# A hybrid encoder: the combination of three attention groups asked for later and spread between an item's stages, the gates' tanh and product taken apart, and a recurrence's output products six matmuls later

## The chip, the cores and the metric

The kernel runs on one core of one Trainium2 chip. The time is that of one execution on the device in microseconds, and smaller is better. The core has a matrix engine (TensorE, PE), a vector engine (VectorE, DVE), an activation engine (ScalarE, ACT), a general one (GpSimd, POOL), and SyncE (SP), which here only issues transfers. Each engine takes its own instructions strictly in order; semaphores hold an instruction back until what it needs is there.

## The reference, cut to what matters

Two request groups (1024 and 512 tokens of width 1024) go through two layers. Layer 0 is attention in three dilated groups, whose outputs are combined by a softmax over their log-sum-exps, times a SiLU gate. Layer 1 is a bidirectional complex-diagonal state-space recurrence in 64 groups.

```
def dilated_mixer(h, w_in, w_out):
    proj = h @ w_in
    z = proj[..., 3 * N_DIL * ATTN_WIDTH:]
    for g, (window, dil) in enumerate(DILATED_PAIRS):
        ...
        q = apply_rope(qkv[:, :, 0], cos, sin) * scale
        k = apply_rope(qkv[:, :, 1], cos, sin)
        o, lse = dilated_window_attention(q, k, v, dil, window // (2 * dil))
        outs.append(o)
        lses.append(lse)
    weights = jax.nn.softmax(jnp.stack(lses, axis=0), axis=0)
    o = jnp.einsum('gbsh,gbshe->bshe', weights.astype(h.dtype), jnp.stack(outs, axis=0))
    y = o.reshape(bsz, s, ATTN_WIDTH) * jax.nn.silu(z)
    return y @ w_out

def s5_mixer(...):
    ...
    _, states = lax.associative_scan(_linear_recurrence, (a, bu), axis=1, reverse=(direction == 1))
    y = y + jnp.real(jnp.einsum('bsgp,gcp->bsgc', states, c_mat))
    g = jax.nn.gelu(y)
    y = g * jax.nn.sigmoid(g @ w_glu)
    return (y * jax.nn.silu(z)) @ w_out
```

## The kernel before

**Order of work.** The program writes its order out by hand. A `Timeline` holds items; one item is a block of 24 matmuls of a projection on TensorE (`gemm`, the tile `mm`), with 25 places ("slots") between them. `H(item, slot, function)` hangs a piece of other work at a slot, and the pieces are emitted there, in this order, on whichever engines they use. So a slot number sets the place of an instruction in the queue of its engine, not its time. A slot beyond 24 is counted on into the following items: slot 199 of an item is slot 24 of the seventh item after it.

**Layer 0.** The 16 heads are worked in eight pairs p. For each pair come group 0, group 1, group 2 (12 items each, T = 0 to 11) and then three items of the gate z ("group 3", units (p, 3)). Each attention item hangs its own chain into the items behind it: rope at slot 24 (VectorE's products `t`, GpSimd's sums, L899 and L900, and later the values `ve` and `vs`), the transposed queries and keys at 38 (TensorE's `qkT`, ScalarE's copies, VectorE's low parts `qT` and `kT`, L969 and L971, and GpSimd's casts `kT`), scores `sc` at 76, softmax at 79, transposed weights `eT` and `et` from 100, the product with the values `pv` at 118, and six matmuls later ScalarE's `pw` and `u` and GpSimd's add of `u` (L1082). In the steady stretch, one item after the other, several such chains interleave. The weights of a next unit come as raw tiles (`wraw`, SyncE, L829) and are split into a high part (ScalarE, `whl`, L841) and a low part (VectorE or GpSimd, L844). `u01` and `U` hold the three groups' outputs of a pair; the next pair's group 1 writes its columns of them item by item.

**Combination of a pair.** Once the last item of group 2 has its softmax sums, `combine_load` fetches the statistics of all three groups (`cst`). `combine_prep` has three parts: the minimum and the exponential (ScalarE, `cd`), the division, and a transposition (TensorE, tile `ada`) whose copy `ft` is stored to DRAM; then `f_load` asks for the coefficients `f` of the first chunk, spread over the partitions, in two halves. The tile `f` (128 x 3 x 512) exists once. `combine` treats the tokens in three chunks c = 0, 1, 2 of 512, each in four parts: part 0 multiplies `f` by group 1's output (VectorE, L1165), part 1 by group 0's (VectorE, L1168) and adds (GpSimd, L1169), part 2 by group 2's (VectorE, L1178) and adds (GpSimd, L1179), part 3 multiplies by the gate into `y` (VectorE, L1185), stores `y`, and asks for the next chunk's `f`. This runs beside the next pair's group 1, for p = 0 to 6; the last pair's combination is part of the output projection (`out_proj0`) and hangs elsewhere.

**Gates.** `stage_silu` of a gate item computes tanh on ScalarE into `zs` and right behind it a product on VectorE.

**Layer 1.** For each of the 64 recurrence groups, twelve matmuls apart, `layer1` hangs five steps: inputs `s_b` (0), `s_pre` (1), the scan `s_scan` (9), `s_post` (18) and the output products `s_y` (30), which read the states `sS`. A GLU and an output projection follow.

**Output projection of layer 0.** `out_proj0` hangs the splitting of eight weight blocks (`w_cvt`, L1460 on VectorE) between the last pair's combination parts.

Of the kernel before, what the change touches and what calls it, by code (L numbers as in the profile page):

```python
# [10 lines left out]
F32 = mybir.dt.float32  # L11
# [3 lines left out]
AF = mybir.ActivationFunctionType  # L15
ALU = mybir.AluOpType
# [4 lines left out]
KT = 8  # L21
# [119 lines left out]
class Kern:  # L141
# [550 lines left out]
    def attention(self):  # L692
        nc, I, tl = self.nc, self.I, self.tl
        H = tl.hook
# [8 lines left out]
        for u, (p, g) in enumerate(units):  # L703
            first = at_unit[p, g] = len(tl.items)
            n = NT if g < 3 else 3
            for T in range(n):
                if u == 0 and T < 2:
                    tl.idle(1)
                    i = T
                else:  # L710
                    i = tl.add(self.gemm, (p, g, T))
                if g < 3:
# [6 lines left out]
                    for nm, (ds_, sl) in at.items():  # L719

                        ds_, sl = at[nm] = divmod(max(25 * ds_ + sl, end_of), 25)
# [4 lines left out]
                    if T == NT - 1:  # L726
                        st = divmod(25 * at["soft"][0] + at["soft"][1] + LATER["soft"][0], 25)
                        H(i + st[0], st[1], self.stats_out, p, g)
                        if g == 0:
                            H(i + at["pv"][0] + (at["pv"][1] + LATER["pv"][1] + 1) // 25, (at["pv"][1] + LATER["pv"][1] + 1) % 25, self.u0_store, p)  # L730
                        if end:
                            H(i + st[0], st[1], self.combine_load, p)
                            for k, sl in enumerate((4, 10, 16)):
                                H(i + 3, sl, self.combine_prep, p, k)
                        elif g == 2:
                            H(i + st[0], st[1], self.combine_load, p)
                            for k, sl in enumerate((110, 120, 135)):
                                H(i + sl // 25, sl % 25, self.combine_prep, p, k)
                            for c in range(3):
                                for k, (ds_, sl) in enumerate(((0, 10), (0, 22), (1, 14), (1, 24))):  # L740
                                    H(i + 6 + 3 * c + ds_, sl, self.combine, p, c, k)
                            H(i + 16, 2, self.u0_load, p + 1)
                elif u + 1 < len(units) or T < n - 1:
                    H(i, 24, self.stage_silu, p, T)
            last = i
            if u + 1 == len(units):
                continue
# [350 lines left out]
        dst = D_[1024:1536].rearrange("(i r) c -> i r c", r=4)[:, :, 4 * g:4 * g + 4]  # L1098
        nc.sync.dma_start(dst, st[:, 8:12].rearrange("p r a b -> p r (a b)"))

    def stage_silu(self, p, c):

        nc, A, B = self.nc, self.pools.get("A"), self.pools.get("B")
        ps = self.state.pop(("ps", (p, 3, c)))
        th = self.sb(self.pools["B"], [128, 512], F32, "zs", bufs=3)
        nc.scalar.activation(th, ps, AF.Tanh, scale=0.5)
        nc.vector.scalar_tensor_tensor(th, th, 1.0, ps, op0=ALU.add, op1=ALU.mult)
        self.zs[(p, c)] = th

    def combine_load(self, p):  # L1110
        sc = self.sb(self.pools["B"], [128, NT, 3, 2, 2], F32, "cst", bufs=1)
# [294 lines left out]
    def out_proj0(self):  # L1406


        nc, I, tl = self.nc, self.I, self.tl
        H = tl.hook  # L1410
# [88 lines left out]
        ps = {}  # L1499
# [62 lines left out]
        H(z, 24, y_cvt, 8, nc.vector, 4, P)  # L1562
        H(z, 24, y_cvt, 9, None, 4, P)
        H(z, 24, gates)
        for k, sl in zip(range(2, KT), (0, 8, 21, 35, 47, 52)):
            H(base + sl // 25, sl % 25, w_cvt, k)
        H(base + 47 // 25, 47 % 25, y_cvt, 10)
        H(base + 54 // 25, 54 % 25, y_cvt, 11)
# [59 lines left out]
    def layer1(self):  # L1628

        nc, I, tl = self.nc, self.I, self.tl  # L1630
        H = tl.hook
# [314 lines left out]
            at(T0 + 4 * R * hb - (26 if hb < 2 else 46), u_load, hb)  # L1946
            at(T0 + 4 * R * hb + 3 * R + 44, g_store, hb)
        for g in range(64):
            for off, fn in ((-24, par_load), (0, s_b), (1, s_pre), (9, s_scan), (18, s_post), (30, s_y)):
                at(T0 + R * g + off, fn, g)  # L1950

        def s_end():
# [10 lines left out]
        for n, T in enumerate(order):  # L1963
            s = base6 + 2 * n
            for h in range(2):
                if T == last and h == 1:
                    i = tl.add(lambda m: [mm_last(1 + m // 12, 2 * (m % 12) + e) for e in range(2)])
                else:
                    i = tl.add(mm1, T, h)
# [49 lines left out]
```

## Time and profile before

| | |
|---|---|
| median of 3 runs | 3045.18 us (3042.79 to 3051.17) |
| the profiled execution's own time | 3043.34 us |
| its span, first to last instruction | 3041.2 us |
| TensorE busy | 2771.2 us (91% of the span) |
| VectorE busy | 2149.5 us (71%) |
| ScalarE busy | 1700.9 us (56%) |
| GpSimd busy | 1618.1 us (53%) |
| mean granted TensorE clock | 0.976 of full speed |

Busy shares are averages over stages. What a change in one stage is worth is read from the waits in that stage. In the rows further down, a number in square brackets is the time for which the engine had stood idle before the instruction, with what ended the idle time; an instruction without a bracket followed its predecessor.

### The profile page before, as it was taken

Reading aid. Unit: us, or ns where it says so; the run is one execution under the profiler, and the core shown is the slowest. Engines: PE = TensorE matmul, PEld = TensorE weight load, DVE = VectorE, ACT = ScalarE, POOL = GpSimd, SP = SyncE. Lnnn points to the kernel's source line nnn. Section 1 sums busy time; section 2 is a strip of 40 time slices with the busy share of each in tenths; the row PEclk is TensorE's granted clock in tenths of the full one; section 3 lists DMA queues with packets and bytes.
Section 4 is the critical chain, followed back from the end, with each engine's and each line's share of the span. In section 5 each row is a group of like instructions: output and inputs, shape, how many; then the busy total and the mean of one; then the engine's idle time right before and its main releaser. Section 6 shows DMA issues by size and latency. Waiting matters only on the chain. (4 is left out here: it accounts for less than half of the span.)

```text
span 3041.2 us, 52468 instructions
## 1 busy us (share of the span) xinstructions
PE 2771.2 (91%) x16181; PEld 2414.7 (79%) x16181; DVE 2149.5 (71%) x6071; ACT 1700.9 (56%) x5120; POOL 1618.1 (53%) x2657
## 2 busy tenths in 40 slices
PE   6899999997898989989898998989899998889998
PEld 5798888886787878888787888888688666567887
DVE  7777887775875767677676767767643889975345
ACT  5876777777665757656565666756453222223221
POOL 3765655555764545556464645546463665542243
PEclk8999999998999999999999999999999999999999
DMA  7122333321222222222212122122644554536454
GB/s 210 58 85 85 93 91 89 91 81 29 60 69 70 60 59 63 59 56 57 69 44 73 50 69 65 51 59 55 170 132 134 182 164 149 163 130 190 161 158 132
DMA packets 428232, 293.78 MB, mean 97 GB/s; under 512 B 140288, under 2 KB 379152, under 8 KB 427824
## 3 DMA queue, kind: packets, MB, share of 16 engines
q1 hardware_dynamic: 427808, 290.16, 33.5%
q8 instruction: 129, 2.11, 0.3%
q14 instruction: 151, 1.24, 0.1%
q10 hardware_dynamic: 144, 0.26, 0.0%
HBM read 204.72 MB, written 85.62 MB: 95 GB/s over the span
## 5 line engine op out<-in xcount | busy, mean ns | idle before, releaser
L886 PE MATMUL mm<-whl,hp 128*128 128x384 f32 x4584 | 999.7, 355 | 4.7 <-ACT hp L356 2.8
L886 PEld LDWEIGHTS mm<-whl,hp 128*128 128x128 f32 x4584 | 809.3, 198 | 24.5 <-issue 11.5
L886 PE MATMUL mm<-whl,hs 128*128 128x384 f32 x2304 | 492.0, 347 | 0.0
L886 PEld LDWEIGHTS mm<-whl,hs 128*128 128x128 f32 x2304 | 393.4, 190 | 7.5 <-issue 7.2
L975 POOL CAST kT<-kT 64x128 fp32r<-64x128 f32 x576 | 171.4, 298 | 359.3 <-ACT kT L966 340.1
L969 DVE SCALAR_TENSOR_TENSOR qT<-qkT,qT 64x128 fp32r<-64x128 f32 x576 | 166.2, 289 | 271.3 <-ACT kT L966 265.2
L1082 POOL TENSOR_TENSOR u<-u,pw 128x128 f32<-128x128 f32 x384 | 184.7, 481 | 217.2 <-ACT u L1078 201.6
L1649 PE MATMUL mm<-hp,wi 128*128 128x512 f32 x1104 | 279.5, 401 | 1.8 <-ACT sig L1686 1.8
L1010 ACT ACTIVATE e<-e,st 128x128 f32<-128x128 f32 (+2 forms) x576 | 249.4, 435 | 48.3 <-DVE st L1025 43.6
L1649 PEld LDWEIGHTS mm<-hp,wi 128*128 128x128 f32 x1104 | 202.6, 188 | 53.3 <-issue 8.6
L1077 ACT ACTIVATE pw<-pv 64x256 f32<-64x256 f32 x576 | 218.0, 378 | 46.9 <-PE pv L1068 30.5
L964 ACT ACTIVATE qT<-qkT 64x128 fp32r<-64x128 f32 x576 | 156.3, 271 | 150.7 <-PE qkT L952 144.4
L951 PE MATMUL qkT<-ident,t 128*128 128x128 f32 x288 | 89.1, 309 | 124.4 <-POOL t L900 122.8
L899 POOL TENSOR_TENSOR t<-t,t 128x128 f32<-128x128 f32 x288 | 138.6, 481 | 87.7 <-DVE t L916 71.3
L951 PEld LDWEIGHTS qkT<-ident,t 128*128 128x128 f32 x288 | 40.6, 141 | 174.9 <-POOL t L900 173.4
L942 ACT ACTIVATE vs<-mm 64x128 fp32r<-64x128 f32 (+1 forms) x350 | 95.9, 274 | 148.5 <-DVE t L916 145.7
L1055 DVE TENSOR_TENSOR et<-eT,et 128x512 fp32r<-128x512 f32 (+1 forms) x288 | 163.6, 568 | 14.9 <-ACT et L1053 14.9
L971 DVE TENSOR_TENSOR kT<-qkT,kT 64x128 fp32r<-64x128 f32 x576 | 166.2, 289 | 9.8
L1348 DVE TENSOR_TENSOR f<-f,p_pb 128x4 f32<-128x4 f32 (+6 forms) x448 | 163.6, 384 | 4.0 <-POOL f L1337 0.9
L1053 ACT ACTIVATE et<-eT 128x512 fp32r<-128x512 f32 (+1 forms) x288 | 144.7, 503 | 38.4 <-PE eT L1043 27.6
L841 ACT ACTIVATE whl<-wraw 128x384 fp32r<-128x384 f32 (+1 forms) x224 | 112.6, 507 | 95.8 <-DMA wraw<-in_attn_w_in 91.5
L966 ACT ACTIVATE kT<-qkT 64x128 fp32r<-64x128 f32 x576 | 156.8, 272 | 10.6
(367 smaller groups left out, 6259.7 us busy)
## 6 DMA issues: line engine op xcount, KB each, us to landing
wraw<-in_attn_w_in SPq DMA_DIRECT2D x192, 192.0 KB
par<-par_d SPq DMA_DIRECT2D x64, 512.0 KB
f<-f_d SPq DMA_DIRECT2D x44, 384.0 KB
par_d<-zs SPq DMA_DIRECT2D x64, 256.0 KB
U<-in_ada_w SPq DMA_DIRECT2D x16, 768.0 KB
par_d<-f SPq DMA_DIRECT2D x64, 128.0 KB
raw<-in_ssm_w_in SPq DMA_DIRECT2D x14, 512.0 KB
u_d<-u SPq DMA_DIRECT2D x8, 768.0 KB
```

Of the source, the lines that this page charges most:

```text
L886: nc.tensor.matmul(ps[:, :384], self.hv(a, k, self.tok_cols(g, T)), self.wt[((p, g), k)][:, b], start=m == 0, stop=m == 23)
L964: nc.scalar.activation(qT[r, h], tp[r, 0:128], AF.Copy, scale=-0.125)
L966: nc.scalar.activation(kT[r, 0, h, c], tp[r, 128:256], AF.Copy)
L969: nc.vector.scalar_tensor_tensor(qT[o, h], tp[r, 0:128], -0.125, qT[r, h].bitcast(F32), op0=ALU.mult, op1=ALU.subtract)
L971: nc.vector.tensor_tensor(kT[r, 1, h, c], tp[r, 128:256], kT[r, 0, h, c].bitcast(F32), op=ALU.subtract)
L975: nc.gpsimd.tensor_copy(kT[o, 0, h, c], kT[r, 0, h, c].bitcast(F32))
L1010: nc.scalar.activation(e[:, h, :W], e[:, h, :W], AF.Exp, scale=-1.0, bias=st[:, T, h, 0:1], accum_out=st[:, T, h, 1:2])
L1055: nc.vector.tensor_tensor(et[:, 1, 0:n], tp[:, 0:n], et[:, 0, 0:n].bitcast(F32), op=ALU.subtract)
L1077: nc.scalar.activation(w[hi], pv[hi, h], AF.Copy)
L1082: nc.gpsimd.tensor_tensor(u, u, w[:, a], op=ALU.add)
L1348: v.tensor_tensor(o, x, y, op=op)
L1649: nc.tensor.matmul(st["ps"], state[("w", u)][a][:, k], self.hv(b, k, slice(512 * c, 512 * c + 512)), start=m == 0, stop=m == 23)
```

## The change

Slot numbers change for `combine_prep`, `combine`, one `w_cvt` and `s_y`, and `stage_silu` is called in two halves. No computation is added or removed.

```
 elif g == 2:
     H(i + st[0], st[1], self.combine_load, p)
-    for k, sl in enumerate((110, 120, 135)):
+    for k, sl in enumerate((120, 134, 145)):
         H(i + sl // 25, sl % 25, self.combine_prep, p, k)
     for c in range(3):
-        for k, (ds_, sl) in enumerate(((0, 10), (0, 22), (1, 14), (1, 24))):
-            H(i + 6 + 3 * c + ds_, sl, self.combine, p, c, k)
+        for k, sl in enumerate(((184, 195, 209, 220), (245, 270, 295, 309), (345, 370, 384, 395))[c]):
+            H(i + sl // 25, sl % 25, self.combine, p, c, k)
...
-    H(i, 24, self.stage_silu, p, T)
+    H(i, 24, self.stage_silu, p, T, 0)
+    H(i + 1, 8, self.stage_silu, p, T, 1)
```

```
 # out_proj0, weight blocks 2 to 7
-for k, sl in zip(range(2, KT), (0, 8, 21, 35, 47, 52)):
+for k, sl in zip(range(2, KT), (0, 8, 9, 35, 47, 52)):
     H(base + sl // 25, sl % 25, w_cvt, k)
 # layer1
-for off, fn in ((-24, par_load), (0, s_b), (1, s_pre), (9, s_scan), (18, s_post), (30, s_y)):
+for off, fn in ((-24, par_load), (0, s_b), (1, s_pre), (9, s_scan), (18, s_post), (36, s_y)):
     at(T0 + R * g + off, fn, g)
```

Written as slots from the last item of group 2, `combine` stood at 160, 172, 189, 199 for chunk 0, at 235, 247, 264, 274 for chunk 1, and at 310, 322, 339, 349 for chunk 2. In `stage_silu`, half 0 is the tanh and half 1 the product; the last pair's last gate item still calls both at once. After the change the lines from 1083 on stand one to two further down, so L1165 of before is L1167 of the change, L1168 is L1170, L1169 is L1171, L1179 is L1181, L1185 is L1187, L1082 is L1083 and L844 is L845.

The first place is VectorE's queue where the coefficients of the first pair leave: `ft` is their copy, `qT` and `kT` are the low parts of an item's queries and keys, and `t` are rope's products of the next. Before:

```order
1940 L1141 COPY ft<-ada 72x128
1941 L969 SCALAR_TENSOR_TENSOR qT<-qkT,qT 64x128 x2
1942 L971 TENSOR_TENSOR kT<-qkT,kT 64x128 x2
1943 L915 TENSOR_TENSOR t_12817<-mm,rope 128x256
1944 L916 TENSOR_TENSOR t_12818<-mm,rope 128x256
```

and now:

```order
1940 L970 SCALAR_TENSOR_TENSOR qT<-qkT,qT 64x128 x2
1941 L972 TENSOR_TENSOR kT<-qkT,kT 64x128 x2
1942 L1143 COPY ft<-ada 72x128
1943 L916 TENSOR_TENSOR t_12817<-mm,rope 128x256
1944 L917 TENSOR_TENSOR t_12818<-mm,rope 128x256
```

The copy, and with it the store and the load of `f` behind it, moved behind the low parts.

The second place is VectorE's queue from chunk 0's part 3 (`y`) to chunk 1's part 0 (L1165, later L1167) of the same pair; `e,st` rows of the softmax stand in the gaps. Before:

```order
1963 L1185 SCALAR_TENSOR_TENSOR y<-f,zs 128x512
1964 L915 TENSOR_TENSOR t_12943<-mm,rope 128x256
...
1973 L969 SCALAR_TENSOR_TENSOR qT<-qkT,qT 64x128 x2
1974 L971 TENSOR_TENSOR kT<-qkT,kT 64x128 x2
1975 L915 TENSOR_TENSOR t_13024<-mm,rope 128x256
...
1983 L895 TENSOR_TENSOR vs<-mm,vs 64x128
1984 L1165 TENSOR_TENSOR f<-f,u_693 128x512
1985 L969 SCALAR_TENSOR_TENSOR qT<-qkT,qT 64x128 x2
```

and now:

```order
1974 L1187 SCALAR_TENSOR_TENSOR y<-f,zs 128x512
1975 L916 TENSOR_TENSOR t_13024<-mm,rope 128x256
...
1983 L896 TENSOR_TENSOR vs<-mm,vs 64x128
1984 L970 SCALAR_TENSOR_TENSOR qT<-qkT,qT 64x128 x2
1985 L972 TENSOR_TENSOR kT<-qkT,kT 64x128 x2
1986 L1167 TENSOR_TENSOR f<-f,u_693 128x512
1987 L916 TENSOR_TENSOR t_13108<-mm,rope 128x256
```

Part 3 stands one item later than before against the same rope pieces (`t_13024`), part 0 a few rows later; so one item's pieces lie between the two where there were one and a half.

The third place is GpSimd's queue at the end of chunk 2 of the first pair, where a weight tile is split (`whl`). Before, both of chunk 2's adds (L1169, L1179) stood further up:

```order
783 L899 TENSOR_TENSOR t_13447<-t_13447,t_13448 128x4x32
784 L900 TENSOR_TENSOR t_13447<-t_13447,t_13448 128x4x32
785 L975 CAST kT<-kT 64x128 x2
786 L1082 TENSOR_TENSOR u_693<-u_693,pw 128x128 x2
787 L899 TENSOR_TENSOR t_13525<-t_13525,t_13526 128x4x32
788 L900 TENSOR_TENSOR t_13525<-t_13525,t_13526 128x4x32
789 L844 TENSOR_TENSOR whl<-wraw,whl 128x384
790 L975 CAST kT<-kT 64x128 x2
```

and now:

```order
783 L976 CAST kT<-kT 64x128 x2
784 L1171 TENSOR_TENSOR f<-f 128x512
785 L1083 TENSOR_TENSOR u_693<-u_693,pw 128x128 x2
786 L900 TENSOR_TENSOR t_13520<-t_13520,t_13521 128x4x32
787 L901 TENSOR_TENSOR t_13520<-t_13520,t_13521 128x4x32
788 L1181 TENSOR_TENSOR f<-f 128x512
789 L845 TENSOR_TENSOR whl<-wraw,whl 128x384
790 L976 CAST kT<-kT 64x128 x2
```

Part 1's add stands ahead of the item's `u` adds, and part 2's add directly ahead of the split of the weight tile.

## Rows read from the trace of the kernel before

**Rows 1.** Waits of TensorE and VectorE, 928 to 2110 us: total, times, longest.

```profile
PE qkT L951 <- POOL t L900: 80.9, 81, 3.4
PE sc L999 <- DVE kT L971: 13.4, 7, 3.0
...
DVE f L1165 <- DMA f<-f_d: 18.6, 8, 3.5
```

**Rows 2.** Order of time on TensorE, first pair: start, duration, instruction.

```profile
951.24 0.33 PE L951 MATMUL qkT<-ident,t 128*128 128x128 f32 x1 [0.84 <-POOL t L900]
...
961.67 0.68 PE L999 MATMUL sc<-kT,qT 128*128 128x192 f32 x3 [3.04 <-DVE kT L971]
...
966.51 0.33 PE L951 MATMUL qkT<-ident,t 128*128 128x128 f32 x1 [2.04 <-POOL t L900]
...
979.23 0.27 PE L951 MATMUL qkT<-ident,t 128*128 128x128 f32 x1
...
986.79 0.33 PE L951 MATMUL qkT<-ident,t 128*128 128x128 f32 x1 [1.61 <-POOL t L900]
...
1006.11 0.33 PE L951 MATMUL qkT<-ident,t 128*128 128x128 f32 x1 [1.66 <-POOL t L900]
...
1012.00 0.33 PE L951 MATMUL qkT<-ident,t 128*128 128x128 f32 x1
...
1025.61 0.48 PE L951 MATMUL qkT<-ident,t 128*128 128x128 f32 x1 [2.48 <-POOL t L900]
```

**Rows 3.** Order of time on VectorE, first pair.

```profile
947.00 0.20 DVE L1123 TENSOR_TENSOR cM<-cst 128x24 f32<-128x24 f32 x1 [1.94 <-DMA cst<-st_d]
...
951.47 0.29 DVE L1141 COPY ft<-ada 72x128 f32<-72x128 f32 x1
...
953.50 0.59 DVE L971 TENSOR_TENSOR kT<-qkT,kT 64x128 fp32r<-64x128 f32 x2
...
959.68 1.04 DVE L1165 TENSOR_TENSOR f<-f,u 128x512 f32<-128x512 f32 x1 [3.53 <-DMA f<-f_d]
...
961.97 0.69 DVE L1168 TENSOR_TENSOR f<-f,u 128x512 f32<-128x512 f32 x1
...
969.45 1.11 DVE L1185 SCALAR_TENSOR_TENSOR y<-f,zs 128x512 f32<-128x512 f32 x1
...
978.98 1.09 DVE L1165 TENSOR_TENSOR f<-f,u 128x512 f32<-128x512 f32 x1
```

**Rows 4.** Order of time on GpSimd, first pair.

```profile
978.44 0.46 POOL L900 TENSOR_TENSOR t<-t,t 128x128 f32<-128x128 f32 x1
...
982.86 1.29 POOL L1169 TENSOR_TENSOR f<-f 128x512 f32<-128x512 f32 x1 [1.21 <-issue]
984.11 1.01 POOL L1082 TENSOR_TENSOR u<-u,pw 128x128 f32<-128x128 f32 x2
...
1017.23 1.01 POOL L844 TENSOR_TENSOR whl<-wraw,whl 128x384 fp32r<-128x384 f32 x1
```

**Rows 5.** Order of time on ScalarE, first pair.

```profile
947.79 0.26 ACT L1127 ACTIVATE cd<-cd 128x72 f32<-128x72 f32 x1 [3.51 <-DVE cd L1126]
```

**Rows 6.** Order of time on SyncE, first pair: the issue of two loads of `f`.

```profile
953.29 1.29 SPq L1153 DMA_DIRECT2D f<-f_d  x2
...
971.12 1.24 SPq L1153 DMA_DIRECT2D f<-f_d  x2
```

**Rows 7.** DMA engines from 968 to 982 us, busy tenths in 40 slices.

```profile
DMA  0000000000888899149999853100000000001000
```

**Rows 8.** Stretch behind the last stop: length, busy times, TensorE's granted clock, DMA.

```profile
1025.20:1028.60 3.40, 2.99 (x11) 3.00 (x12) 1.06 (x4) 1.77 (x6) 2.85 (x5) 0.52 0.27 39
```

**Rows 9.** Waits of VectorE in the recurrence, 2350 to 2724 us.

```profile
DVE sW L1755 <- POOL sA L1746: 32.7, 64, 1.3
```

**Rows 10.** Stretch behind the recurrence: length, busy time of TensorE (matmuls), and the others.

```profile
2724.00:2840.00 116.00, 114.17 (x503) 93.74 (x502) 51.82 (x61) 35.52 (x55) 27.78 (x19) 1.00 0.61 178
```

**Rows 11.** Order of time on VectorE, output projection of layer 0.

```profile
2169.04 2.29 DVE L1460 TENSOR_TENSOR wo<-s_hp,wo 128x1024 fp32r<-128x1024 f32 x1
```

**Rows 12.** Order of time on TensorE, output projection of layer 0.

```profile
2171.39 2.50 PE L1506 MATMUL sc<-wo,hs 128*128 128x512 f32 x5 [5.46 <-DVE wo L1460]
```

More of the change, by code (lines that the diff above doesn't have):

```diff
@@ L1099, in stats_out, with stage_silu @@
         nc.sync.dma_start(dst, st[:, 8:12].rearrange("p r a b -> p r (a b)"))
-    def stage_silu(self, p, c):
+    def stage_silu(self, p, c, part=None):
         nc, A, B = self.nc, self.pools.get("A"), self.pools.get("B")
[L1104 to L1108, printed above, removed]
+        if part != 1:
+            self.zs[(p, c)] = self.sb(self.pools["B"], [128, 512], F32, "zs", bufs=3)
+            nc.scalar.activation(self.zs[(p, c)], self.state["ps", (p, 3, c)], AF.Tanh, scale=0.5)
+        if part != 0:
+            th = self.zs[(p, c)]
+            nc.vector.scalar_tensor_tensor(th, th, 1.0, self.state.pop(("ps", (p, 3, c))), op0=ALU.add, op1=ALU.mult)
     def combine_load(self, p):
```

## The prediction

> **What bounds the kernel now.** I read three views of the profile in this order: what TensorE waits for, the order of time on each engine through one head pair, and then the DMA traffic there. The stretch from 928 to 2110 us holds seven head pairs of about 173 us each. In it TensorE's long stops hang on two producers: VectorE's and GpSimd's rope pieces, 80.9 us before `qkT` and 13.4 us before `sc` [rows 1]. TensorE is the bound, since between these stops its matmuls follow one another, so a stop that appears or goes is time of the whole kernel. The stops of the first pair stand one under the other [rows 2]: 0.84 us at 951.24, 3.04 at 961.67, 2.04 at 966.51, 1.61 at 986.79, 1.66 at 1006.11 and 2.48 at 1025.61; the `qkT` at 979.23 and 1012.00 in between waited for nothing. The other pairs repeat them. One item of 25 slots lasts about 5.8 us there (1006.11 to 1012.00, less the stop's tail, is 5.89).
>
> What causes each is seen on the engine ahead of it:
> - 3.04 and 2.04: VectorE stands still until chunk 0's `f` has landed, 3.53 us in this pair [rows 3], 18.6 us over the seven (the third of [rows 1]). Everything queued behind the first product (the `qT`/`kT` lows, then rope) is late by this.
> - 1.61 and 1.66: GpSimd's add of part 1 (1.29 us) stands ahead of the `u` adds and the rope sums, whose normal lead over `qkT` is only 0.33 us: the sum ends at 978.44 + 0.46 = 978.90, `qkT` starts at 979.23 [rows 2, 4].
> - 2.48: GpSimd frees a raw weight buffer at 1017.23 + 1.01 = 1018.24, SyncE then issues the next raw weights, ScalarE's conversion waits for them, and the `u` writes, the `u` adds and the sums follow [rows 4].
>
> **The change part by part.** The profiled execution lasted 3043.34 us by its own time (span 3041.2); the median of the runs is 3045.18, so a sum made against the profile is put 1.8 us higher at the end.
>
> *Gates' product and group coefficients, 0 us.* The product leaves the place ahead of `et`, and the last coefficient steps leave the place ahead of rope. But the stop that ends at 951.24 comes down another chain: the statistics `cst` land at 947.00, ScalarE's exponential runs at 947.79 (it waited 3.51 us), and only behind it come ScalarE's `pw` and `u`, then GpSimd's adds and sums [rows 3, 5]. The exponential stays ahead of `pw` in ScalarE's order, so the stop ends where it did; what goes from earlier stops of the same chain comes back in this one. If the chain were not bound, at most about 2 us per pair could go.
>
> *Chunk 0, a gain of 3.0 us per pair.* `ft` moves behind the `qT`/`kT` lows, from 951.47 to about 954.1 [rows 3], 2.65 us later; `f` then lands at 959.68 + 2.65 = 962.3. The product that needs it moves 24 slots, 24/25 of 5.8 us, from 956.15 (959.68 less its wait) to 961.7. The wait thus falls from 3.53 to about 0.6 here, and to nearly nothing in the other pairs, whose waits are shorter (18.6 over seven pairs and one late chunk). Before, the two stops cost 13.4/7 = 1.9 plus 2.0. What stays is the add of part 1 ahead of the sums, as in the 1.66 stop, but without the 1.01 us of `u` add, which has not begun at these slots: 0.65, and 0.3 of wait. That is 3.9 less 0.95. Bounds: 1.5 (the load is as late again as `ft`) to 3.9.
>
> *Chunk 1, a loss of 4.8 us per pair.* This is the main term. Its `f` has one buffer, so its load is issued only after part 3 of chunk 0, which ends at 969.45 + 1.11 = 970.56 [rows 3]. The two halves go out at 971.12 [rows 6]. Chunk 0's same two halves needed from 953.29 to 959.68, 6.39 us [rows 3, 6]; so 977.5 here, 6.95 us after part 3's end. The DMA view agrees: its 40 slices of 0.35 us show the engines busy up to slice 26, 977.1 us [rows 7]. Before, part 0 of chunk 1 came at 978.98, 8.4 us after, and waited for nothing. Now it stands 25 slots after part 3 instead of 36: 5.8 less part 3's own 1.11 is 4.7 us. VectorE so waits about 2.1 us, and its rope pieces stand behind the wait and the 1.09 us of product: 2.1 + 1.09 - 0.33 of lead = 2.9, say 3.0 us of stop at the next `qkT`. Bounds: 0.5 (load hidden) to 3.4. Parts 1 and 2, which shared an item, now delay one item each. Part 1 as in the 1.66 stop, but without part 2 beside it: 1.2 (0.85 to 1.66). Part 2 now stands ahead of its own item's rope and `u` adds with a strided product, as long as part 0's 1.04 to 1.09 us, where part 1 has 0.69 [rows 3]: 1.66 + 0.4, with some standing still beside GpSimd 2.2 (1.3 to 2.5). Together 6.4 against the 1.61 that it replaces.
>
> By the Trainium skill, "DMA: Bandwidth & Descriptors", section "Anatomy of one DMA", a transfer takes about 2.0 us plus its bytes at 436 GB/s, 3.8 us for the 786 KB of two halves (an estimate by that page). By it chunk 1's `f` would be back within 5 us and almost nothing would wait. The trace has 6.39 us for these very transfers, so the sum goes by the trace; the page's rate stands for the first rival.
>
> *Chunk 2, 0.* Its load gets 36 slots, 8.3 us, and parts 1 and 2 stand to each other and to rope nearly as before: the 1.66 stays, one item and a half later.
>
> *The stop at 1025.61, a loss of 1.6 us per pair.* Chunk 2's part 2 now falls in the item where GpSimd frees the raw weight buffer, and its add goes ahead of that conversion, as the order shows. An add of 1.29 us, as its sister of part 1 has it [rows 4], behind VectorE's product pushes 1018.24 by about 1.6, and the whole chain behind it (weights, ScalarE, `u`, sums) with it. Bounds 0 (another transfer is last) to 2.2.
>
> *Clock, a loss of 0.7 us per pair.* After the stop at 1025.61 the granted clock was 0.52 for 3.4 us, about half of full speed (1.2 instead of 2.4 GHz) [rows 8], which costs 1.7 us. The new 3.0 us stop is longer than that one and likely draws such a stretch in half of the pairs or more; two pairs lose one behind chunk 0. Bounds 0 to 1.7.
>
> *Recurrence, a gain of 1.4 us, once.* `s_y` six slots later takes TensorE's wait for `sS` away, but in this stretch VectorE's scan sets the pace, and its waits are for GpSimd, 0.5 us in each of 64 groups (32.7 us) [rows 9]. They stay. Only the end gains: work of TensorE worth six matmuls of 114.17/503 = 0.227 us [rows 10] moves across the boundary. Bounds 0 to 3. If the pace were TensorE's, more would go.
>
> *Output projection, a gain of 1.5 us, once.* A weight conversion of 2.29 us on VectorE [rows 11] moves ahead of products, into an idle stretch, where TensorE had waited 5.46 us [rows 12]; the chunks behind it are still bound by products, so less than the 2.29 comes through. Bounds 0 to 2.3.
>
> Sum: seven pairs of -3.0 + 4.8 + 1.6 + 0.7 = +4.1, which is 28.7; less 1.4 and 1.5, **+25.8**. 3043.3 + 25.8 + 1.8 = **3071 us**.
>
> **The rivals.**
> - *Chunk 1's load is hidden.* If the load takes under 5 us, as the page's rate has it, its stop is 0.3 instead of 3.0 and draws no clock stretch: 25.8 - 7 x (2.7 + 0.7) = +2, **3047 us**. For it: the engines show a half-idle stretch between two bursts, part of which may be `yT`'s store. Against: 6.39 us without that store in front. It decides at a wait under 0.3 us.
> - *Faster: the pieces of chunk 1 fall into slack.* If no item of chunk 1 stops TensorE, because GpSimd takes each add before the sums of its item come due, chunk 1 gains its 1.61 and no clock is lost: 7 x (-3.0 - 1.61 + 1.6) - 2.9 = -24, **3021 us**. It decides where a lone add costs less than the lead of 0.33 us. Against: the add lasts 1.29 us, four times the lead, and the 1.66 stop shows it.
> - *The chain of statistics was not the bound.* Then the product's and the coefficients' moves bring up to 2 us per pair: +26 - 14 = +12, **3057 us**. Against: 947.00 is a landing, and ScalarE's order is unchanged.
> - *It does nothing in the recurrence or the projection*: +2.9, inside the range.
>
> **How the numbers follow.** The main case has 0.68, hidden load 0.12, slack 0.11, the other chain 0.09. No change is what stays within 0.3% of 3045, 3036 to 3054. The main case reaches from 3056 to 3087: the upper end adds chunk 0's smaller gain (+10) and a clock stretch in every pair (+7); the lower takes part 2's and the weight chain's lower bounds (6 + 9). The range takes in the hidden load and the other chain, **3047 to 3087**, and leaves out the slack case and the tails. Faster 0.14 (the slack case and some of the combinations), same 0.13, slower 0.73.
>
> **What would show it.** Right: chunk 1's part 0 with a wait of about 2 us for `f`, and a `qkT` stop of about 3 us behind it, in all seven pairs; chunk 0's wait under 1 us and no `sc` stop; two more stops of 1 to 2.5 us where one of 1.61 stood; the stop after the weight chain at about 4 us; the stop that ends with the statistics still at the same distance from the landing of `cst`. Wrong: no wait for `f` at chunk 1, or a landing of the next raw weights that didn't move with GpSimd's conversion.

## The result and the profile after

The changed kernel takes 3070.55 us (median of 4 runs, 3066.20 to 3078.99) beside 3045.99 us before (median of 4): a ratio of 1.0082, 95% interval 1.0055 to 1.0110, so 24.6 us slower. The prediction said 3071. The profiled execution is the slowest of the four, 3078.99 us by its own time (span 3077.2), so sums made from its rows come out some 8 us too high; the second run of the experiments, which has the combination's change alone, is set beside it for that reason.

First the waits of the same stretch of seven head pairs, 930 to 2176 us after the change (total, times, longest), beside [rows 1]:

```profile
PE qkT L952 <- POOL t L901: 78.7, 81, 3.3
...
PE qkT L952 <- DVE ve L896: 19.4, 7, 3.3
...
DVE f L1167 <- DMA f<-f_d: 15.3, 10, 2.4
...
PE sc L1000 <- POOL kT L976: 4.4, 7, 0.7
```

The `sc` wait for VectorE's `kT` of [rows 1] (13.4 us, once in each pair) is gone. A new group of exactly seven stands in its place: `qkT` behind `ve`, 19.4 us, 2.8 us each. (`qkT` itself reads GpSimd's sums `t`, and these end 0.02 to 0.03 us ahead of `ve` in all seven pairs; the view names the one that ended last.) VectorE still waits for `f`, 15.3 us in place of 18.6, but 12.9 of them at chunk 1, where it had waited for nothing.

TensorE's order of time in the first pair, its stops from the statistics on (one of 0.32 us left out), beside [rows 2]:

```profile
953.34 0.33 PE L952 MATMUL qkT<-ident,t 128*128 128x128 f32 x1 [0.56 <-POOL t L901]
...
970.14 0.33 PE L952 MATMUL qkT<-ident,t 128*128 128x128 f32 x1 [1.08 <-POOL t L901]
...
974.28 0.82 PE L1000 MATMUL sc<-kT,qT 128*128 128x192 f32 x4 [0.69 <-POOL kT L976]
...
985.80 0.48 PE L952 MATMUL qkT<-ident,t 128*128 128x128 f32 x1 [2.82 <-DVE ve L896]
...
1001.05 0.33 PE L952 MATMUL qkT<-ident,t 128*128 128x128 f32 x1 [1.95 <-POOL t L901]
...
1020.25 0.33 PE L952 MATMUL qkT<-ident,t 128*128 128x128 f32 x1 [1.83 <-POOL t L901]
...
1029.07 0.33 PE L952 MATMUL qkT<-ident,t 128*128 128x128 f32 x1 [3.26 <-POOL t L901]
```

Chunk 0's two stops of 3.04 and 2.04 us are gone; 1.08 and 0.69 stand there. Chunk 1, where one stop of 1.61 stood, has 2.82 at 985.80 and 1.95 at 1001.05. Chunk 2's 1.83 now comes one item before the stop behind the weights, 3.26.

What holds chunk 1 is in VectorE's order of time, with rope's last product, ScalarE's, GpSimd's and SyncE's rows behind it:

```profile
964.24 1.10 DVE L1167 TENSOR_TENSOR f<-f,u 128x512 f32<-128x512 f32 x1 [0.94 <-DMA f<-f_d]
...
973.03 1.10 DVE L1187 SCALAR_TENSOR_TENSOR y<-f,zs 128x512 f32<-128x512 f32 x1
...
981.72 1.09 DVE L1167 TENSOR_TENSOR f<-f,u 128x512 f32<-128x512 f32 x1 [1.88 <-DMA f<-f_d]
```

```profile
983.19 0.41 DVE L917 TENSOR_TENSOR t<-mm,rope 128x256 f32<-128x256 f32 x1
```

```profile
982.85 0.27 ACT L1079 ACTIVATE u<-pv 64x128 f32<-64x128 f32 x1 [3.56 <-DVE f L1167]
```

```profile
983.94 0.99 POOL L1083 TENSOR_TENSOR u<-u,pw 128x128 f32<-128x128 f32 x2 [4.86 <-DVE st L1026]
984.89 0.45 POOL L900 TENSOR_TENSOR t<-t,t 128x128 f32<-128x128 f32 x1
985.29 0.45 POOL L901 TENSOR_TENSOR t<-t,t 128x128 f32<-128x128 f32 x1
```

```profile
974.15 0.37 SPq L1196 DMA_DIRECT2D yT<-y  x1
974.69 1.24 SPq L1155 DMA_DIRECT2D f<-f_d  x2
```

Part 3 of chunk 0 ends at 974.13 and frees the only tile `f`; the load is issued at 974.69, and its consumer starts at 981.72, 7.6 us after part 3's end. Over the seven pairs VectorE's wait there is 1.67 to 2.43 us. The rows behind it show the way by which the delay reaches TensorE. ScalarE's write of `u` stands still for 3.56 us, because the product still has to read that tile (24.6 us over the seven pairs). GpSimd's `u` adds stand behind that write and its rope sums behind the `u` adds. Rope's products were through at 983.60, 1.3 us before the first sum began, so here the sums did not wait for them.

At the end of chunk 2, GpSimd's order of time, beside the last of [rows 4]:

```profile
1018.94 1.25 POOL L901 TENSOR_TENSOR t<-t,t 128x128 f32<-128x128 f32 x1
1020.16 1.60 POOL L1181 TENSOR_TENSOR f<-f 128x512 f32<-128x512 f32 x1
1021.73 1.00 POOL L845 TENSOR_TENSOR whl<-wraw,whl 128x384 fp32r<-128x384 f32 x1
1022.79 1.59 POOL L976 CAST kT<-kT 64x128 fp32r<-64x128 f32 x2
```

The split of the weights now ends 2.5 us behind the `qkT` at 1020.25. Before, it ended at 1018.24 [rows 4], 0.6 us behind the `qkT` ahead of it, so by this measure 1.9 us earlier:

```profile
1017.64 0.27 PE L951 MATMUL qkT<-ident,t 128*128 128x128 f32 x1
```

Last, busy times by stretch (length; TensorE's matmuls, its weight loads, VectorE, ScalarE, GpSimd; granted clock): the seven pairs before, after, and in the run with the combination alone, and the 3.5 us from the `qkT` at 985.80 on, after:

```profile
928.30:2139.70 1211.40, 1095.08 (x6633) 1007.75 (x6631) 845.03 (x2798) 773.75 (x2607) 644.08 (x1232) 0.98 0.24 59
```

```profile
930.10:2175.40 1245.30, 1114.49 (x6634) 1027.02 (x6632) 842.51 (x2798) 772.13 (x2609) 639.57 (x1232) 0.96 0.23 58
...
985.80:989.30 3.50, 3.50 (x13) 3.50 (x14) 1.52 (x5) 2.05 (x8) 0.57 (x2) 0.51 0.00 0
```

```profile
929.00:2162.00 1233.00, 1105.86 (x6633) 1018.94 (x6631) 842.90 (x2798) 772.22 (x2607) 641.82 (x1232) 0.97 0.23 58
```

The stretch is 33.9 us longer in the profiled execution. 14.5 us of that are idle time (1245.30 - 1114.49 = 130.8, before 116.3), and 19.4 us are the same matmuls taking longer. The second part is the clock: behind a stop of about 2 us or more TensorE often runs for some 3.5 us at a granted clock of about 0.5, as the short window shows (1.2 instead of 2.4 GHz), and loses half of it, 1.7 us. It also did so behind shorter stops that follow each other closely: five times before the change behind the stop of 0.85 us at the statistics, which had one of 1.2 to 2.0 us ahead of it. Going by matmul durations there are 16 such stretches in the seven pairs before, 28 after and 22 in the run with the combination alone (the few of about double length counted twice): 12 and 6 more, 20.5 and 10.3 us, which agrees with the busy times (+19.4 and +10.8).

### The profile page after: what moved, and what is told of

It is laid out like the page before. It is cut to its first block, busy times and chain, and to the rows that moved or that the text cites. A ratio compares the mean times of both kernels' runs of the same rounds, so it can differ in the third digit from the quotient of the medians.

```text
span 3077.2 us, 52441 instructions
## 1 busy us (share of the span) xinstructions
PE 2790.6 (91%) x16181; PEld 2441.7 (79%) x16181; DVE 2146.1 (70%) x6071; ACT 1698.5 (55%) x5120; POOL 1612.5 (52%) x2657
## 5 line engine op out<-in xcount | busy, mean ns | idle before, releaser
L887 PE MATMUL mm<-whl,hs 128*128 128x384 f32 x2304 | 505.0, 353 | 0.0
L887 PEld LDWEIGHTS mm<-whl,hs 128*128 128x128 f32 x2304 | 404.9, 195 | 7.5 <-issue 7.2
L1083 POOL TENSOR_TENSOR u<-u,pw 128x128 f32<-128x128 f32 x384 | 182.5, 475 | 222.1 <-ACT u L1079 172.2
L1651 PE MATMUL mm<-hp,wi 128*128 128x512 f32 x1104 | 269.9, 399 | 2.9 <-ACT sig L1688 2.9
L1069 PE MATMUL pv<-et,vs 128*128 128x256 f32 x704 | 152.0, 295 | 17.9 <-DVE et L1056 16.0
```

Source lines behind the costliest of these rows:

```text
L887: nc.tensor.matmul(ps[:, :384], self.hv(a, k, self.tok_cols(g, T)), self.wt[((p, g), k)][:, b], start=m == 0, stop=m == 23)
L1069: nc.tensor.matmul(pv[:, h], V[key][:, 2 * h:2 * h + 2].rearrange("p a c -> p (a c)"), et[:, :, ci, h], start=ci == 0, stop=ci == len(chun ...
L1083: nc.gpsimd.tensor_tensor(u, u, w[:, a], op=ALU.add)
L1651: nc.tensor.matmul(st["ps"], state[("w", u)][a][:, k], self.hv(b, k, slice(512 * c, 512 * c + 512)), start=m == 0, stop=m == 23)
```

## The experiments

All ratios are to the kernel before, run on the same chip. "Weights stop" is the one behind the split of a weight tile, the last row of TensorE above.

**1. All but the combination.** The changed kernel with the slots of `combine_prep` and `combine` of before.

```
-for k, sl in enumerate((120, 134, 145)):
+for k, sl in enumerate((110, 120, 135)):
...
-    for k, sl in enumerate(((184, 195, 209, 220), (245, 270, 295, 309), (345, 370, 384, 395))[c]):
+    for k, sl in enumerate(((160, 172, 189, 199), (235, 247, 264, 274), (310, 322, 339, 349))[c]):
```

> The coefficients and the combination stand where they stood before; the gates' tanh and product apart, the weight block and the output products of the recurrence stay changed. My theory (all the loss sits in the combination's new places): the loss goes and the two small gains stay, about 3043 us, within 0.3% of before, and the seven stops of chunk 1 with a wait for its coefficients are not there. The rival that the product's move itself lengthens the stop behind the statistics (in the changed kernel its three stops sum to 1 us more per pair): about 3053 us. The rival that the gates' product had held TensorE up: about 3030 us.

Measured: 3043.06 us beside 3042.19, ratio 1.0000 (0.9986 to 1.0014), 11 runs. The gates, the weight block and `s_y` together bring nothing that can be told from zero; the interval leaves room for some 4 us either way.

**2. The combination alone.** `stage_silu`, `w_cvt` and `s_y` as before.

```
-for k, sl in zip(range(2, KT), (0, 8, 9, 35, 47, 52)):
+for k, sl in zip(range(2, KT), (0, 8, 21, 35, 47, 52)):
...
-H(i, 24, self.stage_silu, p, T, 0)
-H(i + 1, 8, self.stage_silu, p, T, 1)
+H(i, 24, self.stage_silu, p, T)
...
-(18, s_post), (36, s_y)
+(18, s_post), (30, s_y)
```

> Only the coefficients and the combination are moved; gates, weight block and recurrence stand as before. My theory: the whole loss, and 3 us more than the full change for the small gains left out, about 3073 us. The rival that the parts need each other for the loss: under 3060 us.

Measured: 3064.40 us, ratio 1.0076 (1.0064 to 1.0089), less than the 3073 us expected. The interval overlaps that of the full change (1.0055 to 1.0110). With run 1: the loss sits in the combination, as far as these intervals can tell.

**3. Chunk 1's load hidden.** The next chunk's `f` is asked for in thirds, each as soon as its third of the tile is free (this holds for chunk 2's load too, for which nothing had waited): the second behind part 1's add, the third behind part 2's add, only the first behind part 3. All slots are those of the change.

```
+    def f_third(self, p, c, g):
+        fd = self.f_d[p].rearrange("(g h t) i -> g h (t i)", g=3, h=2)
+        f = self.state[(p, c - 1, "f")]
+        for h in range(2):
+            src = fd[g, h, 512 * c:512 * c + 512]
...
+            self.nc.sync.dma_start(f[64 * h:64 * h + 64, g], src)
...
+            if p < PAIRS - 1 and c < 2:
+                self.f_third(p, c + 1, 1)
...
+            if p < PAIRS - 1 and c < 2:
+                self.f_third(p, c + 1, 2)
...
-                self.f_load(p, c + 1)
+                self.f_third(p, c + 1, 0)
```

> As the full change, but the next chunk's coefficients come in thirds, each asked for right behind the last use of its third in the chunk before: group 1's third a whole item earlier than now. My theory (the wait for chunk 1's coefficients makes the stop of 2.8 us): VectorE's wait of 1.7 to 1.9 us there goes, the stop falls to about 0.8 us (the product of 1.09 us stays ahead of rope), some clock stretches go with it, 14 to 25 us less than the full change: about 3050 us. The rival that the stop is that of the pieces' order (product ahead of rope, output write held by it), with the load hidden under it: under 5 us, about 3067 us.

Measured: 3049.58 us, ratio 1.0020 (1.0011 to 1.0029), 11 runs. Part 0 of chunk 1 on VectorE and the stops of TensorE in chunk 1, first pair:

```profile
979.88 1.08 DVE L1176 TENSOR_TENSOR f<-f,u 128x512 f32<-128x512 f32 x1
```

```profile
983.96 0.33 PE L952 MATMUL qkT<-ident,t 128*128 128x128 f32 x1 [0.96 <-POOL t L901]
...
991.21 0.33 PE L952 MATMUL qkT<-ident,t 128*128 128x128 f32 x1 [1.27 <-POOL t L901]
...
999.16 0.33 PE L952 MATMUL qkT<-ident,t 128*128 128x128 f32 x1 [1.95 <-POOL t L901]
```

Part 0 waits for nothing and its stop falls from 2.8 to 0.96 us; parts 1 and 2 stop TensorE as before, part 1 now in all seven pairs instead of five. Of the 24.6 us some 18 are gone, and the stretch's busy time of TensorE is back where it was before the change:

```profile
930.70:2146.20 1215.50, 1095.57 (x6633) 1008.42 (x6631) 841.71 (x2798) 772.23 (x2608) 644.36 (x1232) 0.98 0.22 59
```

So the wait for the load, with the clock that it drew, was about three quarters of the loss. What is left, 6 us, is put down to the pieces' places.

**4. Chunk 2's last add behind the split.** Parts 2 and 3 of chunk 2 six and five slots later, the rest as in the change.

```
-    for k, sl in enumerate(((184, 195, 209, 220), (245, 270, 295, 309), (345, 370, 384, 395))[c]):
+    for k, sl in enumerate(((184, 195, 209, 220), (245, 270, 295, 309), (345, 370, 390, 400))[c]):
```

> As the full change, but chunk 2's parts 2 and 3 stand 6 and 5 slots later, so that GpSimd splits the weight tile first and adds afterwards. The prediction's step (the add ahead of the split delays weights, ScalarE and the sums by 1.6 us per pair): 11 us less, about 3059 us. The rival, as the trace of the changed kernel reads (the stop there is 2.1 us, no longer than before, though the add stands ahead of the split): within 4 us of the full change, about 3070 us.

Measured: 3065.15 us, ratio 1.0074 (1.0059 to 1.0089), which can't be told from the change's 1.0082. GpSimd's order of time there, and VectorE's:

```profile
1017.16 1.86 POOL L845 TENSOR_TENSOR whl<-wraw,whl 128x384 fp32r<-128x384 f32 x1
1018.98 1.29 POOL L1181 TENSOR_TENSOR f<-f 128x512 f32<-128x512 f32 x1
```

```profile
1016.81 1.32 DVE L1180 TENSOR_TENSOR f<-f,U 128x512 f32<-128x512 f32 x1
```

The add is behind the split, as meant, but the split itself takes 1.86 us where it took 1.01 [rows 4], because part 2's product runs on VectorE at the same time. It ends 1.8 us behind the `qkT` ahead of it instead of 2.5, and from that `qkT` to the one behind the weights it is still 9.0 us in the mean of the seven pairs, as in the change (before: 1025.61 - 1017.64 = 8.0). So this run does not decide between its two theories; the next one does. By the Trainium skill, "SBUF — State Buffer", section "Who interferes with whom", a VectorE instruction with two inputs in SBUF contends with a GpSimd instruction that reads SBUF, and the ports that they share are an exclusive lock. These rows agree: the product ends at 1018.13, and the split ends 0.89 us after that, nearly its own 1.01.

**5. Part 2 and its add behind the whole item.**

```
-    for k, sl in enumerate(((184, 195, 209, 220), (245, 270, 295, 309), (345, 370, 384, 395))[c]):
+    for k, sl in enumerate(((184, 195, 209, 220), (245, 270, 295, 309), (345, 370, 400, 405))[c]):
```

> As the full change, but chunk 2's parts 2 and 3 stand 16 and 10 slots later, so that neither the product nor the add of part 2 is beside or ahead of the splits of the weight tiles (in the run with the add behind the split, the product ran beside the split and doubled its 1.0 us). Theory now: GpSimd's split then ends 0.6 us behind the item's sums as before instead of 1.8 to 2.5 us, and the distance between the two sums' matmuls around the weights falls from 9.0 to 8.0 us: 7 us less than the full change, about 3062 us. The rival (the landing of the weights doesn't hang on the split): distance 9 us, time as the full change.

Measured: 3084.47 us, ratio 1.0140 (1.0120 to 1.0160). TensorE and VectorE in the first pair:

```profile
1019.06 0.33 PE L952 MATMUL qkT<-ident,t 128*128 128x128 f32 x1 [1.33 <-POOL t L901]
...
1027.05 0.48 PE L952 MATMUL qkT<-ident,t 128*128 128x128 f32 x1 [2.42 <-POOL t L901]
...
1031.38 0.80 PE L1069 MATMUL pv<-et,vs 128*128 128x256 f32 x2 [2.04 <-DVE et L1056]
```

```profile
1029.22 1.77 DVE L1187 SCALAR_TENSOR_TENSOR y<-f,zs 128x512 f32<-128x512 f32 x1 [4.07 <-POOL f L1181]
```

The distance between the two `qkT` did what was expected: 1027.05 - 1019.06 = 8.0 us, as before the change (8.0 to 8.2 in six pairs, 8.8 in one). So chunk 2's part 2 and its add were what made it 9.0. The time did not, since part 3 then stood on VectorE for 4.07 us waiting for GpSimd's add, with the next `et` queued behind it, and TensorE stopped 2.04 us more for that `et`.

**6. The pieces where nobody is late for them.** Thirds as in run 3, `combine_prep` as before, and products and adds at slots of their own: in chunks 0 and 1 a product at slot 10 of an item (ahead of the item's transposed queries and keys) and its add at slot 19 (behind GpSimd's casts).

```
+PLACES = ((185, 0, 0), (185, 0, "1p"), (194, 0, "1a"), (210, 0, "2p"), (219, 0, "2a"), (235, 1, 0), (235, 0, 3),
+          (285, 1, "1p"), (294, 1, "1a"), (310, 1, "2p"), (319, 1, "2a"), (335, 2, 0), (335, 1, 3),
+          (385, 2, "1p"), (385, 2, "2p"), (394, 2, "1a"), (395, 2, "2a"), (401, 2, 3))
```

> Coefficients where they stood before, thirds as in the run with thirds, and every product of the combination at the slot ahead of an item's queries and keys, where VectorE stood idle for 1.8 us, and every add apart from its product, behind the casts, where GpSimd stood idle for 1.6 us. My theory (it is not the amount of combination work but products ahead of rope and adds ahead of the sums that stop TensorE): the stops of chunks 0 to 2, some 7 us per pair in the run with thirds, fall to about 2 us, the stops behind the statistics and behind the weights stay: 35 to 45 us under before, about 3003 us. The rival that what is saved returns in the stop behind the weights, since their landing doesn't come earlier: 3025 us or more.

Measured: 2986.69 us beside 3047.22, ratio 0.9803 (0.9790 to 0.9817). Waits and busy times of the seven pairs:

```profile
PE qkT L954 <- POOL t L903: 50.7, 55, 3.7
...
PE ada L1143 <- DVE cd L1139: 9.9, 6, 3.2
```

```profile
928.60:2083.40 1154.80, 1079.67 (x6633) 1005.03 (x6631) 838.98 (x2798) 771.46 (x2607) 636.71 (x1232) 0.98 0.24 62
```

The expected 3003 us was far too cautious. With the same products and adds the stretch is 56.6 us shorter than before the change: 41.2 us less idle time and 15.4 us less of busy time. In all seven pairs chunks 0 and 1 cause no stop of TensorE at all; of chunk 2 the weights stop remains, 3.6 us.

**7. The same with the exponential behind the output write.** `combine_prep` at 127, 134 and 145, so that ScalarE's exponential stands behind its `pw`.

```
-for k, sl in enumerate((110, 120, 135)):
+for k, sl in enumerate((127, 134, 145)):
```

> As the run with windows, but the exponential of the statistics stands behind ScalarE's output write instead of ahead of it, and the transposition of the coefficients ten slots later. My theory (the stop that ends 4.3 us after the landing of the statistics comes from ScalarE waiting in order at the exponential): that stop falls by about 2 us per pair, 15 us less than the run with windows, about 2988 us; the distance of 4.3 us from the landing is gone. The rival that another chain ends the stop at the same time, or that the wait moves to chunk 0's coefficients: within 5 us of the run with windows.

Measured: 2980.37 us, ratio 0.9780 (0.9763 to 0.9797): 6 us less than run 6, where more was expected, and the two intervals overlap. VectorE and TensorE behind the landing of the statistics, first pair:

```profile
948.62 0.20 DVE L1127 TENSOR_TENSOR cM<-cst 128x24 f32<-128x24 f32 x1
```

```profile
950.21 0.33 PE L954 MATMUL qkT<-ident,t 128*128 128x128 f32 x1
...
952.58 0.31 PE L1143 MATMUL ada<-ident,cd 128*72 128x128 f32 x1 [0.71 <-DVE cd L1139]
...
967.25 0.33 PE L954 MATMUL qkT<-ident,t 128*128 128x128 f32 x1 [0.62 <-POOL t L903]
```

The next `qkT` comes 1.6 us after VectorE's first use of the statistics and stops for nothing; before the change it was 951.24 - 947.00 = 4.24 us, with a stop [rows 2, 3]. Adding TensorE's stops from the pair's beginning to chunk 0, they fall from 3.6 us per pair in run 6 to 2.0, the one before `ada` included (run 6 had it as well). Part of that comes back: a `qkT` of chunk 0, which stopped for nothing in run 6, now stops for 0.6 to 1.05 us in every pair, as the last row shows.

**8. Adds right behind their products.** As run 6, with each add at its product's slot.

```
-PLACES = ((185, 0, 0), (185, 0, "1p"), (194, 0, "1a"), (210, 0, "2p"), (219, 0, "2a"), ...
+PLACES = ((185, 0, 0), (185, 0, "1p"), (185, 0, "1a"), (210, 0, "2p"), (210, 0, "2a"), ...
...
-          (385, 2, "1p"), (385, 2, "2p"), (394, 2, "1a"), (395, 2, "2a"), (401, 2, 3))
+          (385, 2, "1p"), (385, 2, "1a"), (385, 2, "2p"), (385, 2, "2a"), (401, 2, 3))
```

> As the run with windows, but each add right behind its product again, ahead of the casts. My theory (what counts is that product and add are through before the item's output write, rope and sums come): an add of 1.3 us then only pushes the casts by about half a microsecond, which the scores see, 4 to 8 us over seven pairs: about 2993 us. The rival that the adds' own place carried the gain: 3010 us or more.

Measured: 2999.60 us beside 3043.57, ratio 0.9856 (0.9837 to 0.9875).

```profile
PE qkT L954 <- POOL t L903: 58.8, 57, 4.8
```

```profile
1009.20 1.65 DVE L847 TENSOR_TENSOR whl<-wraw,whl 128x384 fp32r<-128x384 f32 x1
```

```profile
1008.34 3.66 POOL L1186 TENSOR_TENSOR f<-f 128x512 f32<-128x512 f32 x2 [0.63 <-DVE f L1181]
```

This is some 13 us more than run 6 (16 by the ratios), where 4 to 8 were expected. No stop came back in chunks 0 and 1, so there the adds need not stand apart. What grew is the weights stop, from 3.6 to between 4.6 and 4.8 us. GpSimd's own split still stands ahead of chunk 2's adds. But these adds now run beside VectorE's split of its weight tile, which takes 1.65 us in every pair where run 6 has 0.65, and the raw weights that are loaded behind it are asked for 1.0 us later.

**9 and 10. Chunk 2 around the split.** As run 7, with chunk 2 behind its item's split in the one (first added line), and only its part 2 there in the other (second).

```
-(385, 2, "1p"), (385, 2, "2p"), (394, 2, "1a"), (395, 2, "2a"), (401, 2, 3)
+(396, 2, "1p"), (397, 2, "1a"), (397, 2, "2p"), (398, 2, "2a"), (405, 2, 3)
+(385, 2, "1p"), (394, 2, "1a"), (397, 2, "2p"), (397, 2, "2a"), (405, 2, 3)
```

> As the run with the exponential behind the output write, but chunk 2's parts 1 to 3 stand behind the splits of the weight tiles on both engines, in the time for which these engines wait for the weights anyway. Theory now: VectorE's split, which stood behind 2.4 us of products there, frees its raw buffer earlier, the stop before the weights falls from 3.6 to about 2.5 us: 7 us less, about 2973 us. The rival (only GpSimd's split counts, which was not late there): same time, 2980 us.

> As the run with the exponential behind the output write, but of chunk 2 only part 1 stays ahead of the splits (0.7 us on VectorE, its add behind the casts), and part 2 with its add goes behind the next queries and keys. Theory now (the stop before the weights is ended by whichever is last: VectorE's split behind products, or GpSimd's adds ahead of the output adds; the run with all of chunk 2 behind traded the one for the other): neither is last here, the stop falls from 3.6 to about 2.8 us, 5 us less, about 2975 us. The rival (any work moved there costs the same): 2980 to 2986 us.

Measured: 2986.04 us, ratio 0.9811 (0.9796 to 0.9826), and 2976.89 us, ratio 0.9783 (0.9768 to 0.9798). In run 9 GpSimd's two adds together became the last to end,

```profile
1014.18 3.58 POOL L1186 TENSOR_TENSOR f<-f 128x512 f32<-128x512 f32 x2 [1.62 <-DVE f L1181]
```

and the weights stop is 4.1 us in all seven pairs where 2.5 was expected. In run 10 it is 3.4 to 3.8 in six pairs and 4.4 in one, where 2.8 was expected, and the time can't be told from run 7's. Its GpSimd and VectorE rows show why, first pair:

```profile
1014.08 1.17 POOL L902 TENSOR_TENSOR t<-t,t 128x128 f32<-128x128 f32 x1
```

```profile
1013.87 1.11 DVE L1204 SCALAR_TENSOR_TENSOR y<-f,zs 128x512 f32<-128x512 f32 x1
```

Part 3 now runs on VectorE just when GpSimd's last pieces before the `qkT` run, and in every pair one of these, a sum or a `u` add, takes 1.2 to 1.3 us for its 0.45. Without this the stop would be 2.6 to 3.0 us in six pairs (an estimate from these rows). Both expectations missed: in neither place was chunk 2 out of the way of both engines.

## Why the prediction was right, step by step

Per head pair, in us, predicted and measured. The stops are sums of TensorE's brackets by place, less those of before; the clock is the busy time of the windows above, divided by seven.

| step | predicted | after, profiled | combination alone |
|---|---|---|---|
| up to the statistics' stop | 0 | +1.0 | +0.3 |
| chunk 0 | -3.0 | -2.6 | -2.5 |
| chunk 1 | +4.8 | +3.9 | +3.5 |
| chunk 2 and the weights stop | +1.6 | -0.2 | 0.0 |
| clock | +0.7 | +2.8 | +1.5 |
| sum | +4.1 | +4.9 | +2.8 |

The stretch itself grew by 4.8 and 3.1 us per pair; the rest is smaller stops outside these places.

- **Chunk 1, the main term,** came nearly as predicted, 3.9 and 3.5 us for 4.8: a wait of 1.7 to 2.4 us for `f` (2.1 said, though its working, 6.95 less 4.7, gives 2.25) and a stop of 2.6 to 3.4, 2.8 in the mean (3.0 said), in all seven pairs, then 1.26 in five of them (two with the combination alone; 1.2 said for all) and 1.95 (2.2 said). Run 3 shows that the load is the cause of the first: with it hidden the wait is gone. The page of the Trainium skill that the prediction weighed ("DMA: Bandwidth & Descriptors", "Anatomy of one DMA") would have it land in 3.8 us (an estimate by that page, whose fit is for transfers that GpSimd issues, which the prediction did not say; SyncE issues these). Here it took 7.0 us from its issue to its consumer's start (974.69 to 981.72), and the trace was right to decide. One part of the step was wrong: it let the delay reach TensorE through VectorE's rope. The path that ended last ran through ScalarE's write of `u`, which could not overwrite what the late product still had to read, then GpSimd's `u` adds and sums. By rope alone the two sums, 0.85 us together, could have ended some 1.3 us earlier, and the stop would have been about 1.5 us (an estimate from the rows of chunk 1). So the cause was right, and that the size came so near was in part luck.
- **Chunk 0** gained 2.5 to 2.6 of the 3.0. The wait fell to 0.94 us in the first pair (0.6 said), and a stop of 0.7 before `sc` stayed.
- **Chunk 2 and the weights stop** was mis-sized, and together with the clock. From the `qkT` ahead of the weights to the one behind them it takes 9.0 us in the mean, 8.0 before: +1.0 where +1.6 was said, inside its bounds; run 5 took this away again. The raw weights moved with GpSimd's split, as the prediction had it: ScalarE's second conversion of them starts 4.9 us behind the `qkT` ahead of them in the first pair, 4.1 before. But the stop itself did not grow to the 4 us that was to show it. In ten of the fourteen pairs of the table's two kernels the new stop of 1.83 one item earlier draws a stretch at half clock, the work between the two takes 1.7 us longer, and the weights stop is shorter by about that: 1.55 to 1.95 us where such a stretch lies between (2.74 in one pair), 3.1 to 3.4 where none does. What the step put down as a stop arrives as clock, in these pairs.
- **Clock** was the step that failed in size: 1.5 to 2.8 us per pair for 0.7. The price of one stretch (1.7 us) was right; the number wasn't. (Behind chunk 0 three stretches went, not the two that were counted.) The 3 us stop draws one in 2 of seven pairs after and in 5 with the combination alone, half of the fourteen as was said; but the shorter new ones draw them as well, the 1.95 in 6 and 2 pairs, the 1.83 in 6 and 4.
- **Statistics, 0:** the mechanism held. In all seven pairs of both kernels the `qkT` stop ends 4.2 to 4.3 us after VectorE first uses `cst`. The profiled execution's +1.0 is not a longer way from there: the landing of `cst` and the stops ahead of it vary from pair to pair (VectorE first uses `cst` 2.5 to 4.4 us after its issue there, 2.5 to 3.6 before), and the kernel with the combination alone has +0.3. What makes them vary was not traced. Run 7 moved the exponential behind `pw`, and there the bound went away.
- **Recurrence and projection:** from the start of the first `sc` to that of the last `pv` of the recurrence it is 370.7 to 371.4 us in the ten kernels with the new slot of `s_y`, 371.2 and 370.9 in the two with the old one. The 1.4 us predicted at its end were not found; a difference under 1 us could hide. The projection, from the transposition of the last pair's coefficients to the first `eT`, takes 51.5 and 51.2 us in the two kernels with the weight block's old slot and 49.1 to 50.7, 49.9 in the mean, in the ten with the new one: the 1.5 us said.

So the total was hit with two misses of opposite sign in it: the stops came to less than predicted (chunk 1 and the weights), the clock to more. That 3071 lies within 1 us of the median is luck: the changed kernel's own runs span 13 us, and the combination alone cost 22 us where 28.7 were said.

**The rivals.** A hidden load did not happen, but its price was near: run 3, which hides it, is at 1.0020, 6 us, and the rival said +2. The pieces of chunk 1 did not fall into slack; that they can is shown by run 6, with other slots. That the statistics were not the bound is refuted by the constant 4.2 to 4.3 us, and by run 7.

**Open.** Run 6's stretch has 15.4 us less of busy time than before the change, but only 4 stretches at half clock fewer (12 for 16, 6.8 us); the other 8.6 us were not tested. The traces offer a reason for most of them: the matmul ahead of a stop counts as busy up to its own end, 0.33 us, where in a dense row the next one begins after 0.17 to 0.18 us (twelve in a row take 2.27 us). Run 6's stretch has 87 stops (idle over 0.05 us) and the one before the change 123, which makes some 6 us (an estimate from these figures). What would make the weights stop short was not found.

## What to carry to other kernels

When side work is spread out over a pipeline, what counts here is not its amount but what is queued behind each piece. The same products and adds gave a ratio of 1.0082 ahead of rope and of the sums, 1.0020 there with the load in thirds, and 0.980 with the load in thirds and in slots where the engines' next piece isn't due. With a single buffer, look first at the distance from its last reader to its next one: it fell to 25 slots, 5.8 us of work, against a load of about 7, and that was about three quarters of the loss. A late reader also holds up whoever writes next into what it reads, as ScalarE's `u` shows. Asking for each part of the buffer behind its own last use took the wait away. And price a new stop of TensorE with the clock behind it: a stop of about 2 us can cost 1.7 us more.

## What the runs showed of the hardware that was not expected

- GpSimd's operations stretch beside VectorE products that read two tiles: the split of a weight tile 1.86 us for 1.01 (run 4), a rope sum 1.25 for 0.46 and two casts 1.59 for 0.64 (the changed kernel). It goes the other way too: VectorE's split takes 1.65 us for 0.65 beside GpSimd's adds (run 8). An order that puts a piece "out of the way" on one engine can slow another.
- A stretch at half clock cost nothing where the next stop was set by another chain: the weights stop was 1.55 to 1.95 us behind one in nine of ten pairs, 3.1 to 3.4 without.
- The same load of statistics reaches VectorE 2.5 to 4.7 us after its issue (4.7 in run 7), and the runs of one kernel lie up to 22 us apart (run 1: 3031.89 to 3054.28).
